# A layer kernel's paired FFN products: a weight split ahead of the last product, another order at the last job's end, sums on GpSimd, and two small products from parts

## The chip, the cores and the metric

The kernel runs on one core of one Trainium2 chip. The metric is the device time in microseconds (us) of one execution. The engines of a core are called PE (TensorE, matrix products), DVE (VectorE), ACT (ScalarE), POOL (GpSimd) and SP (SyncE, which here only issues loads and stores). Each engine works through its own list of instructions in order, and waits where an instruction needs another engine's result. SBUF is the memory of 128 partitions that the engines work on; PSUM has eight banks, in which products add up.

## The reference

One layer of a streaming encoder, on x of 512 rows by 1024 columns in float32:

```python
def swiglu(x, w1, w3, w2):
    return (jax.nn.silu(x @ w1) * (x @ w3)) @ w2

f = swiglu(rms_norm(h, ffn1_pre_g), ffn1_w1, ffn1_w3, ffn1_w2)       # FFN 1
h = h + 0.5 * rms_norm(f, ffn1_post_g)
u = rms_norm(h, mix_pre_g)
...                                   # the mixer: recurrent branch, attention with a
bias = table[t5_bucket(j - 128 - i)]  # relative bias from a table of 32 x 16, gates, w_o
...
f = swiglu(rms_norm(h, ffn2_pre_g), ffn2_w1, ffn2_w3, ffn2_w2)       # FFN 2
h = h + 0.5 * rms_norm(f, ffn2_post_g)
```

w1 and w3 are 1024 x 2816, w2 is 2816 x 1024. 2816 columns are 22 blocks of 128.

## The kernel before, in words

**Products from parts.** Float32 products are made from two parts. `split2` (L191) writes a high part by an ACT copy to the type float32r (L193, "whi" or "hT" in the profile), and the low part as the difference on DVE (L194, "wlo"). A product then is three float32r matmuls: high by high, low by high, high by low. Weights that need no more than that are split by `split_to` (L151), whose lines are L158 (ACT) and L159 (DVE). Loads go by SP, in the order of one long list of weights (`dma_one`, L139). There are 42 buffers of 4 KB a partition, "slots"; a slot is taken again when its last reader is done.

**Pairs of blocks.** The first blocks of w1 and w3 (4 of each in FFN 1, 2 of each in FFN 2) are plain products with 512 columns, L203 to L205. All others go through the class `Pairs` (L476 to L606). One job takes two blocks of w1 (name w1a in FFN 1, w1b in FFN 2) or of w3 (w3a, w3b), as a 2 x 2 matrix of halves, and makes it with 7 products where plainly there are 8. FFN 1 has 18 such jobs, FFN 2 has 20; jobs of w1 and w3 take turns, w1 first. One of the 7 products, `mm_s` (L464), is 12 matmuls with 256 columns (L471 to L473). The 7 need sums of the weights' quarters a11, a12, a21, a22 (and sums of x, made once, t1 to t4):

- S12: two sums (L517, L518), made by POOL, from a21, a22, a11
- S34: two sums (L522, L523), made by DVE, from a12 and S12, and from a11 and a21

The method `prep(m, i)` issues the preparation of job m in five steps: 0 the two sums of S12; 1 the split of the first block, which has a11 and a12; 2 the sums of S34 and the split of S12, which gives s1 and s2; 3 the split of S34, which gives s3 and s4; 4 the split of a22. A step that was already issued is left out when it is called again.

**The order inside a job.** `run` (L534) writes the order by hand. In job n, PE makes a11, s1, then a22 of the job before (function `last`, L591), s2, a12 (c11, L565), s4, s3. Between them stand the copies out of PSUM on ACT (L550, L553, L559, L579, into the tile "ct") and adds on DVE (L568, L573, L580, L585, L586), and the next job's preparation: prep(n+1, 1) right behind `last`, prep(n+1, 2) behind s2, prep(n+1, 3) behind s4, prep(n+1, 4) and prep(n+2, 0) at the job's end. `last` of a w1 job in FFN 1 also copies out of PSUM on ACT (L594) and multiplies the whole job by the norm's factor Rb on DVE (L595); the silu (L596) follows behind s4's add. Rb is handed to `Pairs` in FFN 1 alone (`self.R`); in FFN 2 the norm's factor is in x already. `last` of a w3 job ends with one product on DVE (L603).

In the last job, c11 is made behind s3, and ahead of it `tail()` is called, behind s2: it splits the first two tiles of the hidden layer (`hid.to`, "hT") and the first two blocks of w2, in turn, ACT before DVE in each. In FFN 1 `silu()` of that job comes behind s4, as in the others.

**Two small products.** `root` and `factor` (L708, L714) make Rb: the rows' 512 factors are put on four diagonals (DVE, L712, "dgs") and spread over all partitions by products of float32 ones with them (L717). It stands between plain products of FFN 1. `bias_in` and `bias_rows` (L725, L730) make the bias rows from the table: POOL loads a one-hot matrix 32 x 384 and the table 32 x 16 in job 1, and in job 3 one float32 product (L733) gives 16 x 384, which ACT copies out (L735, "erow"). Such additions to the jobs are handed in as `hooks`, by job and place. Two tiles named gap and gap2 hold memory and are not used.

Of the kernel before, what the change touches and what calls it, by code (L numbers as in the profile page):

```python
# [15 lines left out]
P = 128  # L16
# [6 lines left out]
N_HEADS = 16  # L23
# [28 lines left out]
def hybrid_layer(ctx: ExitStack, tc: tile.TileContext, a: dict, out: bass.AP):  # L52
# [32 lines left out]

    veps = cp.tile([P, NT], F32, name="veps")

    cp.tile([P, 172], F32, name="gap")
    sm.tile([P, 256], F32, name="gap2", bufs=1)
    uT = cp.tile([P, 2, KT, SEQ], F32R, name="uT")  # L90


# [383 lines left out]
    class Pairs:  # L476
# [14 lines left out]
        def prep(self, m, i, eng=None):  # L491
            if m >= len(self.jobs) or (m, i) in self.ready:
                return
            self.ready.add((m, i))
            k = self.k0 + 2 * m
            if i == 0:
                if k not in loaded or k + 1 not in loaded:
                    self.raws(m)
                s12, s34 = slot([P, 2 * QH], name="S12"), slot([P, 2 * QH], name="S34")
                self.w[m] = {"r": (raws.pop(k), raws.pop(k + 1)), "s": (s12, s34)}  # L500
            W = self.w[m]
            (ra, rb), (s12, s34) = W["r"], W["s"]
            a11, a12, a21, a22 = ra[:, :QH], ra[:, QH:], rb[:, :QH], rb[:, QH:]

            def both(src, w=2 * QH):
                hi = slot([P, w], F32R, name="whi")
                lo = slot([P, w], F32R, name="wlo")
                split2(hi, lo, src)
                return hi, lo

            def halves(p, a, b):
                W[a] = p[0][:, :QH], p[1][:, :QH]
                W[b] = p[0][:, QH:], p[1][:, QH:]

            if i == 0:
                e = eng or pool
                e.tensor_tensor(out=s12[:, :QH], in0=a21, in1=a22, op=ALU.add)  # L517
                e.tensor_tensor(out=s12[:, QH:], in0=s12[:, :QH], in1=a11, op=ALU.subtract)  # L518
            elif i == 1:
                halves(both(ra), "a11", "a12")  # L520
            elif i == 2:
                dve.tensor_tensor(out=s34[:, QH:], in0=a12, in1=s12[:, QH:], op=ALU.subtract)  # L522
                dve.tensor_tensor(out=s34[:, :QH], in0=a11, in1=a21, op=ALU.subtract)  # L523
                halves(both(s12), "s1", "s2")
            elif i == 3:
                halves(both(s34), "s3", "s4")
            elif i == 4:
                t = slot([P, 2, QH], F32R, name="w22")
                split2(t[:, 0, :], t[:, 1, :], a22)
                W["a22"] = t[:, 0, :], t[:, 1, :]  # L530
            if all((m, x) in self.ready for x in range(5)):
                del W["r"], W["s"]

        def run(self, tail, hooks={}):  # L534
            X = self.X
            assert st["get"] == st["split"] == self.k0, (st, self.k0)
            st["get"] = st["split"] = self.k0 + 2 * len(self.jobs)
            last = silu = lambda: None
            for n, (nm, f) in enumerate(self.jobs):
                W = self.w.pop(n)  # L540
                first = nm == self.na
                tmp = slot([P, 4, 256], name="ct")
                q1, q5, u, v = (tmp[:, i, :] for i in range(4))
                c = slot([P, 2, SEQ], name="cc")
                if first:
                    self.c1[f] = c
                bu, bx, bc = (bank("c")[:, :256] for _ in range(3))
                at = lambda i: [f() for f in hooks.get((n, i), ())]
                mm_s(W["a11"], X["b11"], bu)
                act.activation(q1, bu, AF.Copy)  # L550
                at(1)
                mm_s(W["s1"], X["t1"], bx)
                act.activation(q5, bx, AF.Copy)  # L553
                at(2)
                silu = last() or silu
                self.prep(n + 1, 1)
                mm_s(W["s2"], X["t2"], bu, True)
                del W["s1"], W["s2"]
                act.activation(u, bu, AF.Copy)  # L559
                at(3)  # L560
                if n == len(self.jobs) - 1:
                    tail()
                self.prep(n + 1, 2)

                def c11():  # L565
                    mm_s(W["a12"], X["b21"], bc)
                    del W["a11"], W["a12"]
                    dve.tensor_tensor(out=c[:, 0, :256], in0=bc, in1=q1, op=ALU.add)  # L568

                if n < len(self.jobs) - 1:  # L570
                    c11()
                mm_s(W["s4"], X["b22"], bx, True)
                dve.tensor_tensor(out=c[:, 0, 256:], in0=bx, in1=u, op=ALU.add)  # L573
                self.prep(n + 1, 3)
                silu()
                silu = lambda: None
                mm_s(W["s3"], X["t3"], bu, True)
                del W["s3"], W["s4"]
                act.activation(v, bu, AF.Copy)  # L579
                dve.tensor_tensor(out=c[:, 1, 256:], in0=v, in1=q5, op=ALU.add)  # L580
                if n == len(self.jobs) - 1:
                    c11()
                if not first:
                    c1 = self.c1[f]
                    dve.tensor_tensor(out=c1[:, 0, :], in0=c1[:, 0, :], in1=c[:, 0, :], op=ALU.mult)  # L585
                    dve.tensor_tensor(out=c1[:, 1, 256:], in0=c1[:, 1, 256:], in1=c[:, 1, 256:], op=ALU.mult)  # L586
                self.prep(n + 1, 4)
                self.prep(n + 2, 0)
                self.raws(n + 3)

                def last(W=W, bu=bu, c=c, f=f, first=first):  # L591
                    mm_s(W.pop("a22"), X["t4"], bu, True)
                    if first and self.R is not None:
                        act.activation(c[:, 1, :256], bu, AF.Copy)  # L594
                        dve.tensor_tensor(out=c, in0=c, in1=self.R, op=ALU.mult)  # L595
                        return lambda: act.activation(c, c, AF.Silu)  # L596
                    if first:
                        act.activation(c[:, 1, :256], bu, AF.Silu)
                        act.activation(c[:, 0, :], c[:, 0, :], AF.Silu)
                        act.activation(c[:, 1, 256:], c[:, 1, 256:], AF.Silu)  # L600
                    else:
                        c1 = self.c1.pop(f)
                        dve.tensor_tensor(out=c1[:, 1, :256], in0=bu, in1=c1[:, 1, :256], op=ALU.mult)  # L603
                        self.hid.f += [c1[:, 0, :], c1[:, 1, :]]

            last()  # L606
# [47 lines left out]
    dma_one(pairs_a.k0)  # L654
    dma_one(pairs_a.k0 + 1)
    make_identity(nc, ident)
    ones = slot([P, P], name="ones")
    pool.memset(ones, 1.0)
    ps = [bank("f") for _ in range(NS)]

    def split_first(u, kp):
# [34 lines left out]
    def t_split(n):  # L696
        X1[f"t{n + 1}"] = to_slots(tg[n])

    dgs = slot([P, NT, P], name="dgs")

    s4 = small(NT, "s4")

    def squares():
        for t in range(NT):
# [3 lines left out]
    def root():  # L708
        r = rstd4(s4)
        act.activation(tiny, tiny, AF.Silu)  # L710
        for t in range(NT):
            dve.tensor_scalar(out=dgs[:, t, :], in0=ident, scalar1=r[:, t : t + 1], scalar2=NEWT, op0=ALU.mult, op1=ALU.mult)  # L712

    def factor():  # L714
        psr = bank("r")
        for t in range(NT):
            pe.matmul(psr[:, t * P : (t + 1) * P], ones, dgs[:, t, :], start=True, stop=True)  # L717
        for i in range(2):
            act.activation(Rb[:, i, :], psr, AF.Copy)

# [2 lines left out]
    oh, erow = [], []  # L723

    def bias_in():  # L725
        oh.append(slot([N_BUCKETS, NREL + 1 + N_HEADS], name="oh"))
        pool.dma_start(out=oh[0][:, : NREL + 1], in_=a["onehot"])
        pool.dma_start(out=oh[0][:, NREL + 1 :], in_=a["rel_bias"])

    def bias_rows():  # L730
        pse = bank("e")
        t = oh.pop()
        pe.matmul(pse[:N_HEADS, : NREL + 1], t[:, NREL + 1 :], t[:, : NREL + 1], start=True, stop=True)  # L733
        erow.append(slot([N_HEADS, NREL + 1], name="erow"))
        act.activation(erow[0], pse[:N_HEADS, : NREL + 1], AF.Copy)  # L735

# [60 lines left out]
    def swiglu(f):  # L797
        t = gates.pop(f)
        hid.f.append(silu_mul(t[:, 0, :], ps[2 * f + 1], t))
# [20 lines left out]
    point(True)  # L820
    xg.clear()
    tg.clear()
    late = {(0, 1): [lambda: swiglu(2)], (0, 3): [lambda: gate(3)], (1, 1): [bias_in, lambda: swiglu(3)], (3, 1): [bias_rows]}
    for i in range(P // 16):
        late[4 + i, 1] = [lambda i=i: bias_spread(i)]

    def w2_ahead():
        hid.to(1)
        split_to(st["split"] + 1)
        hid.to(2)  # L830
        split_to(st["split"] + 1)

    pairs_a.run(w2_ahead, late)
# [460 lines left out]
```

## Time and profile before

| | us |
|---|---|
| median of 3 runs | 1136.61 (1136.0 to 1136.88) |
| profiled execution | 1137.54 |
| its span on the core | 1135.5 |
| PE busy | 1125.4 (99%) |
| DVE busy | 790.0 (70%) |
| ACT busy | 597.8 (53%) |
| POOL busy | 241.1 (21%) |

The page gives the busy time of each engine; PE's clock was granted at nine tenths or more in all of its 40 slices. All times of instructions in this document are counted in us from the span's start. The pairs of FFN 1 stand at about 50 to 237, those of FFN 2 at about 800 to 1005.

A line of the instructions in order of time has the start, the duration, the engine, the line of the program, the operation, what it writes and reads, the shape, and in brackets how long the engine stood idle before it and what ended that. A matmul's record is longer than the step to the next one, because products overlap: a product of 256 columns follows another 0.12 us after it, one of 512 columns 0.227 us. On the other engines the records overlap a little too: an ACT copy of 128 x 1024 lasts 1.06 us as a record and gives way to the next after 0.95; for DVE's subtraction of that size the two are 1.21 and 1.14, for a DVE sum of 128 x 512 they are 0.68 and 0.6.

### The profile page before, as it was taken

To read this page: it belongs to the slowest core of one execution; us is meant where nothing else is said; L and a number is where in the kernel's file an instruction comes from. 1 tells how busy PE (TensorE), PEld (TensorE's weight loads), DVE (VectorE), ACT (ScalarE), POOL (GpSimd) and SP (SyncE) were. 2 spreads that over 40 slices of the span, in tenths; PEclk is the share of its full clock that TensorE was granted. 3 is DMA by queue.
4 is the path that set the end of the run, shared out by engine and by line. 5 is a ranking of instruction groups with operands and counts; after the bars stand their busy time and mean duration, and the time that the engine had idled before them with its cause. 6 is when DMAs were issued, how large, how long until landed. Compare 5 with 4: busy or idle time off the path is not lost.

```text
span 1135.5 us, 17456 instructions
## 1 busy us (share of the span) xinstructions
PE 1125.4 (99%) x6835; PEld 1006.0 (89%) x6835; DVE 790.0 (70%) x1252; ACT 597.8 (53%) x1060; POOL 241.1 (21%) x203
## 2 busy tenths in 40 slices
PE   9999999999999999999999999999999999999997
PEld 7899999988888987888888888889999999998886
DVE  5898989885336747695678865767787777885313
ACT  7755655574324349944656653356555555573211
POOL 0035444200000000001555641000533233300000
PEclk9999999999999999999999999999999999999999
DMA  9235563264313411234122333531333332265101
GB/s 324 96 103 137 122 150 113 75 222 151 110 56 130 149 57 56 75 94 148 56 80 89 93 102 103 187 109 39 111 101 99 100 112 94 74 195 176 38 19 56
DMA packets 37139, 124.95 MB, mean 110 GB/s; under 512 B 4529, under 2 KB 6449, under 8 KB 37057
## 3 DMA queue, kind: packets, MB, share of 16 engines
q1 hardware_dynamic: 34272, 115.15, 30.8%
q0 software_dynamic: 2640, 8.43, 3.8%
q8 instruction: 53, 0.87, 0.3%
q10 hardware_dynamic: 144, 0.26, 0.1%
q14 instruction: 30, 0.24, 0.1%
HBM read 116.50 MB, written 7.33 MB: 109 GB/s over the span
## 4 chain that ended last, share of the span: by engine, by line
PE 91%; DVE 5%; ACT 3%; issue 1%; DMA 0%; SPq 0%; DVEq 0%; ACTq 0%
PE c L472 10%; PE f L203 10%; PE f L204 10%; PE f L205 10%; PE c L473 10%; PE c L471 10%; PE acc L222 8%; PE acc L223 8%; PE acc L221 8%; DVE wlo L194 2%; PE pt L1097 1%; PE s L1061 1%; PE s L1060 1%; DVE S L523 1%; PE tr L313 1%
## 5 line engine op out<-in xcount | busy, mean ns | idle before, releaser
L203 PE MATMUL f<-uT,whi 128*128 128x512 f32 (+1 forms) x472 | 171.7, 364 | 0.0
L204 PE MATMUL f<-uT,wlo 128*128 128x512 f32 (+1 forms) x472 | 170.4, 361 | 0.1
L205 PE MATMUL f<-uT,whi 128*128 128x512 f32 (+1 forms) x472 | 170.1, 360 | 0.0
L221 PE MATMUL acc<-whi,hT 128*128 128x512 f32 x352 | 137.1, 390 | 0.0
L222 PE MATMUL acc<-wlo,hT 128*128 128x512 f32 x352 | 137.0, 389 | 0.0
L223 PE MATMUL acc<-whi,hT 128*128 128x512 f32 x352 | 136.9, 389 | 0.0
L472 PE MATMUL c<-Xh,wlo 128*128 128x256 f32 x456 | 129.8, 285 | 1.1 <-DVE wlo L194 0.6
L471 PE MATMUL c<-Xh,whi 128*128 128x256 f32 x456 | 129.1, 283 | 0.0
L472 PE MATMUL c<-uT,wlo 128*128 128x256 f32 x456 | 129.0, 283 | 0.0
L471 PE MATMUL c<-uT,whi 128*128 128x256 f32 x456 | 129.0, 283 | 0.0
L473 PE MATMUL c<-uT,whi 128*128 128x256 f32 x456 | 129.0, 283 | 0.0
L473 PE MATMUL c<-Xl,whi 128*128 128x256 f32 x456 | 129.0, 283 | 0.0
L193 ACT ACTIVATE whi<-S 128x1024 fp32r<-128x1024 f32 x76 | 80.2, 1057 | 53.0 <-DVE S L523 53.0
L194 DVE TENSOR_TENSOR wlo<-S,whi 128x1024 fp32r<-128x1024 f32 x76 | 101.9, 1341 | 0.3 <-ACT whi L193 0.3
L203 PEld LDWEIGHTS f<-uT,whi 128*128 128x128 f32 x472 | 89.1, 189 | 14.5 <-issue 1.4
L204 PEld LDWEIGHTS f<-uT,wlo 128*128 128x128 f32 x472 | 89.2, 189 | 13.8 <-DVE wlo L159 0.9
L205 PEld LDWEIGHTS f<-uT,whi 128*128 128x128 f32 x472 | 89.1, 189 | 13.5
L472 PEld LDWEIGHTS c<-Xh,wlo 128*128 128x128 f32 x456 | 87.5, 192 | 2.4 <-DVE wlo L194 2.4
L471 PEld LDWEIGHTS c<-Xh,whi 128*128 128x128 f32 x456 | 87.5, 192 | 0.6 <-ACT ct L550 0.6
L471 PEld LDWEIGHTS c<-uT,whi 128*128 128x128 f32 x456 | 87.5, 192 | 0.0
L472 PEld LDWEIGHTS c<-uT,wlo 128*128 128x128 f32 x456 | 87.5, 192 | 0.0
L473 PEld LDWEIGHTS c<-uT,whi 128*128 128x128 f32 x456 | 87.5, 192 | 0.0
(312 smaller groups left out, 2646.8 us busy)
## 6 DMA issues: line engine op xcount, KB each, us to landing
raw_w2a<-in_w2a_dram SPq DMA_DIRECT2D x22, 512.0 KB, 4.4
raw_w1b<-in_w1b_dram SPq DMA_DIRECT2D x22, 512.0 KB, 3.9
raw_w3b<-in_w3b_dram SPq DMA_DIRECT2D x22, 512.0 KB, 4.0
raw_w2b<-in_w2b_dram SPq DMA_DIRECT2D x22, 512.0 KB, 4.4
raw_w3a<-in_w3a_dram SPq DMA_DIRECT2D x21, 512.0 KB, 4.5
raw_w1a<-in_w1a_dram SPq DMA_DIRECT2D x20, 512.0 KB, 4.3
raw_wg<-in_wg_dram SPq DMA_DIRECT2D x16, 512.0 KB, 4.0
raw_xr<-in_xr_dram SPq DMA_DIRECT2D x8, 512.0 KB, 4.0
```

The lines of the kernel that those rows point to most:

```text
L193: act.activation(hi, src, AF.Copy)
L194: dve.tensor_tensor(out=lo, in0=src, in1=f32(hi), op=ALU.subtract)
L203: pe.matmul(ps[:, c0:c1], wh[:, s], h_, start=k == 0, stop=False)
L204: pe.matmul(ps[:, c0:c1], wl[:, s], h_, start=False, stop=False)
L205: pe.matmul(ps[:, c0:c1], wh[:, s], l_, start=False, stop=k == KT - 1)
L221: pe.matmul(acc[n], x[:, 0, c], wh[:, s], start=first, stop=False)
L222: pe.matmul(acc[n], x[:, 0, c], wl[:, s], start=False, stop=False)
L223: pe.matmul(acc[n], x[:, 1, c], wh[:, s], start=False, stop=last)
L313: pe.transpose(ps[:, k * P : (k + 1) * P], hg[:, kk * P : (kk + 1) * P], ident)
L471: pe.matmul(ps, wh[:, s], xh, start=first, stop=False, skip_group_check=True)
L472: pe.matmul(ps, wl[:, s], xh, start=False, stop=False, skip_group_check=True)
L473: pe.matmul(ps, wh[:, s], xl, start=False, stop=k == 3, skip_group_check=True)
```

## The change

1. In FFN 1, prep(n+1, 1), the split of the next job's first block, is issued behind L553, ahead of `last`, and no longer behind it.
2. In the last job, `silu()` is called ahead of `tail()`, and `tail()` is called twice, each time for one tile of the hidden layer and one block of w2: once at the old place, once behind v's add (L580) ahead of c11. The silu is FFN 1's alone, the second call is in both FFNs.
3. In FFN 2, the sums of S34 are issued on POOL, in step 0 of the preparation, behind S12's; in FFN 1 they stay on DVE in step 2. 40 instructions change engine.
4. The factor's product is made in float32r from a high and a low part of the row factors, with 8 diagonals for 4, as two products with 512 columns. The bias product is made likewise, from parts of the table that are split at a new place, behind s2 of job 2 (`bias_parts`).

```diff
-    cp.tile([P, 172], F32, name="gap")
-    sm.tile([P, 256], F32, name="gap2", bufs=1)
+    cp.tile([P, 168], F32, name="gap")
+    sm.tile([P, 240], F32, name="gap2", bufs=1)
...
+            def sums34(e):
+                e.tensor_tensor(out=s34[:, QH:], in0=a12, in1=s12[:, QH:], op=ALU.subtract)
+                e.tensor_tensor(out=s34[:, :QH], in0=a11, in1=a21, op=ALU.subtract)
+
             if i == 0:
                 e = eng or pool
                 e.tensor_tensor(out=s12[:, :QH], in0=a21, in1=a22, op=ALU.add)
                 e.tensor_tensor(out=s12[:, QH:], in0=s12[:, :QH], in1=a11, op=ALU.subtract)
+                if self.R is None:
+                    sums34(e)
             elif i == 1:
                 halves(both(ra), "a11", "a12")
             elif i == 2:
-                dve.tensor_tensor(out=s34[:, QH:], in0=a12, in1=s12[:, QH:], op=ALU.subtract)
-                dve.tensor_tensor(out=s34[:, :QH], in0=a11, in1=a21, op=ALU.subtract)
+                if self.R is not None:
+                    sums34(dve)
                 halves(both(s12), "s1", "s2")
...
                 at(2)
+                if self.R is not None:
+                    self.prep(n + 1, 1)
                 silu = last() or silu
                 self.prep(n + 1, 1)
...
                 if n == len(self.jobs) - 1:
+                    silu()
+                    silu = lambda: None
                     tail()
...
                 if n == len(self.jobs) - 1:
+                    tail()
                     c11()
...
-    ones = slot([P, P], name="ones")
-    pool.memset(ones, 1.0)
+    ones = slot([P, P], F32R, name="ones")
+    pool.memset(f32(ones), 1.0)
...
-    dgs = slot([P, NT, P], name="dgs")
+    dgs = [slot([P, NT, P], F32R, name="dgs") for _ in range(2)]
...
+    tiny_r = [sm.tile([P, NT], F32R, tag="smr", name=f"rn{n}", bufs=2) for n in range(2)]
...
-        for t in range(NT):
-            dve.tensor_scalar(out=dgs[:, t, :], in0=ident, scalar1=r[:, t : t + 1], scalar2=NEWT, op0=ALU.mult, op1=ALU.mult)
+        rh, rl = tiny_r
+        dve.tensor_scalar(out=rh, in0=r, scalar1=NEWT, scalar2=None, op0=ALU.mult)
+        dve.scalar_tensor_tensor(out=rl, in0=r, scalar=NEWT, in1=f32(rh), op0=ALU.mult, op1=ALU.subtract)
+        for x, d_ in zip(tiny_r, dgs):
+            for t in range(NT):
+                dve.tensor_scalar(out=d_[:, t, :], in0=ident, scalar1=f32(x)[:, t : t + 1], scalar2=None, op0=ALU.mult)
...
-        for t in range(NT):
-            pe.matmul(psr[:, t * P : (t + 1) * P], ones, dgs[:, t, :], start=True, stop=True)
+        for n, d_ in enumerate(dgs):
+            pe.matmul(psr, ones, d_.rearrange("p t q -> p (t q)"), start=n == 0, stop=n == 1)
...
-        oh.append(slot([N_BUCKETS, NREL + 1 + N_HEADS], name="oh"))
+        oh.extend((slot([N_BUCKETS, NREL + 1 + N_HEADS], name="oh"), slot([N_BUCKETS, NREL + 1 + 2 * N_HEADS], F32R, name="ohr")))
...
+    def bias_parts():
+        t, u = oh
+        n = NREL + 1
+        hi, lo = u[:, n : n + N_HEADS], u[:, n + N_HEADS :]
+        act.activation(u[:, : n + N_HEADS], t, AF.Copy)
+        dve.tensor_tensor(out=lo, in0=t[:, n:], in1=f32(hi), op=ALU.subtract)
+        oh[:] = [hi, lo, u[:, :n]]
...
-        pe.matmul(pse[:N_HEADS, : NREL + 1], t[:, NREL + 1 :], t[:, : NREL + 1], start=True, stop=True)
+        pe.matmul(pse[:N_HEADS, :n], hi, u, start=True, stop=False)
+        pe.matmul(pse[:N_HEADS, :n], lo, u, start=False, stop=True)
...
-    late = {(0, 1): [lambda: swiglu(2)], (0, 3): [lambda: gate(3)], (1, 1): [bias_in, lambda: swiglu(3)], (3, 1): [bias_rows]}
+    late = {(0, 1): [lambda: swiglu(2)], (0, 3): [lambda: gate(3)], (1, 1): [bias_in, lambda: swiglu(3)], (2, 3): [bias_parts], (3, 1): [bias_rows]}
...
     def w2_ahead():
-        hid.to(1)
-        split_to(st["split"] + 1)
-        hid.to(2)
+        hid.to(hid.done + 1)
         split_to(st["split"] + 1)
```

More of the change, by code (lines that the diff above doesn't have):

```diff
@@ L725, in bias_in @@
     def bias_in():
-        oh.append(slot([N_BUCKETS, NREL + 1 + N_HEADS], name="oh"))
+        oh.extend((slot([N_BUCKETS, NREL + 1 + N_HEADS], name="oh"), slot([N_BUCKETS, NREL + 1 + 2 * N_HEADS], F32R, name="ohr")))
         pool.dma_start(out=oh[0][:, : NREL + 1], in_=a["onehot"])
         pool.dma_start(out=oh[0][:, NREL + 1 :], in_=a["rel_bias"])
+    def bias_parts():
[5 more added lines that the diff above has]
+        oh[:] = [hi, lo, u[:, :n]]
     def bias_rows():
         pse = bank("e")
-        t = oh.pop()
-        pe.matmul(pse[:N_HEADS, : NREL + 1], t[:, NREL + 1 :], t[:, : NREL + 1], start=True, stop=True)
+        hi, lo, u = oh
+        oh.clear()
+        n = NREL + 1
+        pe.matmul(pse[:N_HEADS, :n], hi, u, start=True, stop=False)
+        pe.matmul(pse[:N_HEADS, :n], lo, u, start=False, stop=True)
         erow.append(slot([N_HEADS, NREL + 1], name="erow"))
```

## The prediction

> **What bounds the kernel now.** I read four views in this order: the page (busy times, chain), the waits of the two FFN 1 and FFN 2 stretches, the instructions in order of time around TensorE's pauses, and the stretches by engine.
>
> One line of the page, then waits of two windows, 60 to 240 and 800 to 1005 (waiter, what it waited for, total us, times, longest):
>
> ```profile
> PE 1125.4 (99%) x6835; PEld 1006.0 (89%) x6835; DVE 790.0 (70%) x1252; ACT 597.8 (53%) x1060; POOL 241.1 (21%) x203
> DVE cc L595 <- ACT cc L594: 17.5, 9, 3.1
> PE c L472 <- DVE wlo L194: 0.6, 1, 0.6
> PE c L471 <- ACT ct L579: 0.3, 1, 0.3
> DVE wlo L194 <- ACT whi L193: 38.0, 10, 4.7
> ```
>
> TensorE (PE) is the bound, and only what shortens its stream counts. The second to fourth of the five lines are FFN 1's, the last is FFN 2's. Busy time hides short pauses, because a product's record overlaps the next one. So I take the steps between starts: a 256-column product follows the last by 0.12 us, a 512-column one by 0.227. Wherever a step is longer, time is lost:
>
> ```profile
> 93.12 0.28 PE L471 MATMUL c<-Xh,whi 128*128 128x256 f32 x1
> 93.49 0.39 PE L472 MATMUL c<-Xh,wlo 128*128 128x256 f32 x1
> 93.72 0.28 PE L473 MATMUL c<-Xl,whi 128*128 128x256 f32 x1
> ...
> 234.07 0.28 PE L473 MATMUL c<-uT,whi 128*128 128x256 f32 x1
> 234.66 0.39 PE L471 MATMUL c<-Xh,w 128*128 128x256 f32 x1 [0.31 <-ACT ct L579]
> 234.88 0.28 PE L472 MATMUL c<-Xh,w 128*128 128x256 f32 x1
> ```
>
> At 93.12 two steps take 0.60 instead of 0.24: 0.36 lost, waiting for the low half of the next job's s1. The same stands at 113.62, 134.14 and 154.65: together 1.43. At 234.07, 0.57 is lost. At 61.06 (job 1's s1) 0.85, at 967.71 and 988.09 (FFN 2) 0.22 and 0.34. These are all the pauses over 0.05 in the pair stretches beside the two small products:
>
> ```profile
> 38.98 0.39 PE L205 MATMUL f<-uT,whi 128*128 128x512 f32 x1
> 39.20 1.05 PE L717 MATMUL r<-dgs,ones 128*128 128x128 f32 x8
> 40.01 0.48 PE L203 MATMUL f<-uT,whi 128*128 128x512 f32 x1
> 40.33 0.40 PE L204 MATMUL f<-uT,wlo 128*128 128x512 f32 x1
> 40.56 0.39 PE L205 MATMUL f<-uT,whi 128*128 128x512 f32 x1
> ```
>
> From 38.98 to 40.56 three ordinary steps should take 0.68; they take 1.58, so the factor costs 0.90. The bias product's two L733 records stand between 256-column products that start at 81.98 and 83.28: 1.30 where three ordinary steps would take 0.36, so it costs 0.94.
>
> **Next job's split ahead of the last product (FFN 1).** The chain to the pause at 93.12, on VectorE (DVE):
>
> ```profile
> 86.53 1.23 DVE L595 TENSOR_TENSOR cc<-cc,Rb 128x1024 f32<-128x1024 f32 x1 [2.46 <-ACT cc L594]
> 87.67 2.33 DVE L194 TENSOR_TENSOR wlo<-raw_w1a,whi 128x1024 fp32r<-128x1024 f32 x1
> 89.92 1.78 DVE L522 TENSOR_TENSOR S<-raw_w1a,S 128x512 f32<-128x512 f32 x1
> 91.63 0.68 DVE L523 TENSOR_TENSOR S<-raw_w1a,raw_w1a 128x512 f32<-128x512 f32 x1
> 92.23 1.21 DVE L194 TENSOR_TENSOR wlo<-S,whi 128x1024 fp32r<-128x1024 f32 x1
> ...
> 972.37 4.16 POOL L517 TENSOR_TENSOR S<-raw_w1b 128x512 f32<-128x512 f32 x1 [6.76 <-PE c L472]
> ```
>
> DVE stands idle 2.46 before L595, since L595 needs ScalarE's (ACT's) L594, which needs the last product a22. Then it has no gap to the end. The change puts the split whi (0.95 per step on ACT) behind L553, which starts at 84.68, so at 85.06. That ends at 86.1, and DVE can begin wlo at 86.1 instead of L595 at 86.53. The work behind is the same: wlo 1.14, L595 1.14, two sums 0.6 each, wlo 1.14, and 2.2 of blocking by GpSimd (POOL), 6.85 in all, so it ends at 92.95 instead of 93.4. The pause needs it by 93.24, which leaves 0.3. At 113.62 the gain is 106.5 against 107.04, likewise enough. What is late behind it: L595, L594's bank and the silu L596 move back by up to 0.7; L596 began only at 93.36, five us after L595, and no bank waits. Value -1.43; ends 0 (GpSimd's blocks fall worse and take the 0.45) and -1.43. In the other jobs L603 and the split only change places, and DVE's wait of 17.5 in all is their cover.
> The moved split issues no DMA, and it passes no POOL instruction; SP's order of loads is the same.
>
> The pause at 61.06 stays: its split belongs to job 0, which has no last product ahead of it. DVE has no gap from 42.42 to it but 0.1. Value 0; ends +0.3 and -0.85.
>
> **The last job.** At 234.07 the last product waits for v (L579), which stands on ACT behind hT, whi, hT, whi and the silu, 230.35 to 234.24. Now silu (0.95), hT (0.52) and whi (0.95) stand ahead: 232.77. s3 ends at 232.75, so v is done at 233.2, before c11's end at 234.19. The second hT and whi follow, on ACT until 234.7, on DVE until 236.4; TensorE wants them after c11, a22 and the first 12 products of FFN 1's w2, at 232.75 + 1.44 + 1.44 + 2.72 = 238.4. That is the cover, two us. Value -0.57; ends -0.57 and 0. FFN 2's tail has no pause before, and the same two us of cover: 0.
>
> **Small products.** The factor becomes two 512-column steps, 0.45 instead of 0.90. But DVE builds eight diagonals (0.20 a step) for four, and two 128x4 operations (0.20 each by the neighbouring L251 to L253): 1.2 more from 36.02. It stood idle 0.92 before 37.82, so it falls 0.28 behind, and the split at 42.42, bound by ACT before, by DVE now, gains only 0.30. As DVE has no gap from there to 61.06, that counts: -0.30; ends -0.45 and 0. The bias product becomes two of 384 columns, between 0.12 and 0.227: 0.17 each, 0.35 for 0.94. Value -0.55, for what changing shapes costs; ends -0.59 and 0. Its parts take ACT about 0.5 (erow took 0.48) and DVE 0.16 in job 2, whose table landed at 63.3, thirteen us ahead; DVE then waits for ACT until 77.3, behind it the two sums and s1's split, due at 82.2 and done at 81.3 at the latest.
>
> **FFN 2's sums by GpSimd.** DVE loses 40 instructions of 0.60 a step, 24 us; POOL gains 40 of 1.29 (alone) to 4.16. DVE's operation blocked by a POOL sum takes 1.1 longer (L522 1.78 for 0.68); in 820 to 978 I count 15.3 us of such lengthening for 32 sums, 0.48 each. So DVE gets 24 back and loses 19 to 44, and had 38 us of idle in this stretch (140.2 busy of 178): it does not become the bound. At the pauses its chain shortens: at 962.9 the split of a1, then L522 1.78, L523 0.68 and s1's split, until 967.8. Without the sums, and with POOL's L518 and one added sum blocking 1.1 each, s1's split ends at 966.65. Value -0.56, both pauses; ends -0.56, and the cost in the fourth rival.
> By the Trainium skill, "SBUF — State Buffer", section "Who interferes with whom", a VectorE operation with two SBUF inputs and a GpSimd one that reads SBUF lock each other out for a whole instruction. The rows of 1.1 agree, but only in about every second case; with the rule in every case DVE loses the 44, still less than its idle time, and the sum stays.
> S34 must be there when ACT splits it, at 987.35 for job 18. POOL began that job's sums at 972.37; with two more at the mean of the four rows, 1.84, it ends at 982.5. New waits for S34 on load slots lie over eight us ahead. Two queues are passed. POOL's later sums start later; the only POOL load behind them is FFN 2's gain (L260), issued at 1064.64 and until then 78.5 behind DVE, so it has cover. SP's loads get their slots up to 3 us later (867.83 is one issue) and take 4 to land: about 875, where POOL reads from 877.28. These 2 us are the cover; behind them stands POOL's lead of 4.8 over ACT's split (982.5 to 987.35).
>
> **Sum.** -1.43 - 0.57 - 0.30 - 0.55 - 0.56 = -3.41. The profiled execution took 1137.54 (span 1135.5 and 2.04 around it), so 1134.1; it lies 0.93 above the median of 1136.61, and against that median the forecast is 1133.2.
>
> **Rivals.**
> 1. As summed: 1133.2, from 1132.4 to 1134.2 by factor and bias at either end. For it: every pause has a named last waiter that the edit moves. Chance 0.58.
> 2. Job 1's 0.85 goes too: 1132.3. POOL's L517 at 57.79 slips in just before DVE's L523 at 57.84 and blocks it 1.1; a shift of 0.1 changes who goes first. Against it: both follow TensorE. Chance 0.12.
> 3. The early split gains nothing: DVE was already gapless behind L595, and 0.3 of margin is less than one block of 1.1. The four pauses stay: 1134.6, the same by the bound below. Chance 0.17.
> 4. POOL becomes late, slower. A job gives it 10.08. If its four sums go at 4.16 and three times 2.16, 10.64, it falls back 0.56 a job; the 4.8 of lead is gone after 8.6 jobs, and the other 11.4 lose 6.4: 1136.6 - 2.9 + 6.4 = 1140.1. It decides from 2.5 us a sum; the rows' mean is 1.84. Chance 0.08.
> The Trainium skill's "GPSIMD Engine Reference", "Performance versus the Vector engine", speaks against this move: elementwise work there takes about twice as long. Here 1.30 against 0.68 agrees.
> The rest, 0.05, are mixtures near no change.
>
> **Numbers.** A measurement of this kernel tells 0.2% (2.3 us) from no change: faster is below 1134.3. From 1 nearly all and 2: 0.69 faster; 3, the rest and 1's edge: 0.23 same; 4: 0.08 slower. The range leaves out rival 4 and the outermost edges: 1131.6 (rival 2 with both small products at their best) to 1136.0 (rival 3 with the small products at nothing and part of FFN 2's gain lost).
>
> **What would show it.** DVE's wait before L595 shrinks from 17.5 to under 9, and steps at job 4, 6, 8 and 10's s1 are 0.12. v in the last job starts within 0.2 of s3's end. The factor's record shows two products in 0.45, the bias two in 0.35. POOL's busy time rises by 40 times 1.3 to 2.2, and ACT's split of S34 never waits for POOL. Wrong it would be if pauses over 0.1 stand in FFN 2's jobs with a POOL sum behind them, or new ones in FFN 1's even jobs.

## The result, and the profile after

The changed kernel takes 1132.7 us, median of 7 runs (1132.33 to 1133.73), against 1136.53 of the kernel before in the same series (1135.89 to 1136.88). The ratio is 0.9968, with a 95% interval of 0.9957 to 0.998: faster by 0.32%. The forecast was 1133.2, the range 1131.6 to 1136.0. The profiled execution of the changed kernel, with a span of 1132.0, was the slowest of the seven, 1133.73; why is told below.

The busy times on the page of the changed kernel (us, share of the span, instructions):

```profile
PE 1122.5 (99%) x6829; PEld 1005.0 (89%) x6829; DVE 798.0 (70%) x1219; ACT 597.4 (53%) x1061; POOL 302.9 (27%) x243
```

Its waits in the FFN 1 stretch, 60 to 240 (waiter, what it waited for, total us, times, longest):

```profile
DVE wlo L194 <- ACT whi L193: 12.0, 11, 2.2
...
DVE cc L606 <- ACT cc L605: 3.1, 1, 3.1
...
PE c L472 <- DVE wlo L194: 0.8, 1, 0.8
```

L606 is the multiplication by Rb (L595 before). DVE waited 17.5 us for its input in 9 jobs; now it waits there once, in the last job, where there is no next split. The waiting itself is mostly still there: 12.0 us of it now stand ahead of splits, for ACT's half, a wait that the list of the kernel before does not have. What counts is that the chain behind it starts earlier. Of TensorE's waits in that stretch one is left, job 1's. DVE has 33 instructions fewer and is busy 8 us longer.

The chain on DVE that leads to the place of the first of the four pauses, in the changed kernel, and then TensorE at that place, each in order of time:

```profile
85.27 1.23 DVE L194 TENSOR_TENSOR wlo<-raw_w1a,whi 128x1024 fp32r<-128x1024 f32 x1 [2.23 <-ACT whi L193]
86.42 1.22 DVE L606 TENSOR_TENSOR cc<-cc,Rb 128x1024 f32<-128x1024 f32 x1
87.55 1.78 DVE L516 TENSOR_TENSOR S<-raw_w1a,S 128x512 f32<-128x512 f32 x1
89.26 1.77 DVE L517 TENSOR_TENSOR S<-raw_w1a,raw_w1a 128x512 f32<-128x512 f32 x1
90.96 1.21 DVE L194 TENSOR_TENSOR wlo<-S,whi 128x1024 fp32r<-128x1024 f32 x1
```

```profile
92.35 0.28 PE L471 MATMUL c<-Xh,whi 128*128 128x256 f32 x1
92.47 0.28 PE L472 MATMUL c<-Xh,wlo 128*128 128x256 f32 x1
92.59 0.28 PE L473 MATMUL c<-Xl,whi 128*128 128x256 f32 x1
```

The split now stands ahead of the multiplication. The chain starts at 85.27, where it started at 86.53; TensorE is 0.77 ahead at this place, so DVE is 0.49 earlier against it. GpSimd's sums blocked other DVE operations than before (both sums, not the split of the first block and the first sum), but the total is the same, 2.2 us. The low half of s1 is done at 92.17 and is wanted at 92.47: the margin is 0.3. The steps are 0.12, with nothing lost.

The last job: the ACT instructions in order of time, then TensorE where it lost 0.57 before:

```profile
228.19 1.05 ACT L607 ACTIVATE cc<-cc 128x1024 f32<-128x1024 f32 x1
229.14 0.62 ACT L193 ACTIVATE hT<-sw 128x512 fp32r<-128x512 f32 x1
229.66 1.05 ACT L158 ACTIVATE whi<-raw_w2a 128x1024 fp32r<-128x1024 f32 x1
230.79 0.39 ACT L589 ACTIVATE ct<-c 128x256 f32<-128x256 f32 x1
```

```profile
231.91 0.28 PE L473 MATMUL c<-uT,whi 128*128 128x256 f32 x1
232.03 0.28 PE L471 MATMUL c<-Xh,w 128*128 128x256 f32 x1
232.15 0.28 PE L472 MATMUL c<-Xh,w 128*128 128x256 f32 x1
```

v (L589) starts as s3's last product ends, and its 0.39 are over 0.85 before TensorE goes on behind c11, at 232.03. No step is longer than 0.12.

The small products of the changed kernel on TensorE, the factor and then the bias:

```profile
38.76 0.39 PE L205 MATMUL f<-uT,whi 128*128 128x512 f32 x1
38.98 0.61 PE L733 MATMUL r<-dgs,ones 128*128 128x512 f32 x2
39.44 0.39 PE L203 MATMUL f<-uT,whi 128*128 128x512 f32 x1
```

```profile
81.52 0.28 PE L473 MATMUL c<-uT,whi 128*128 128x256 f32 x1
81.72 0.34 PE L759 MATMUL e<-ohr 32*16 32x384 f32 x1
81.92 0.33 PE L760 MATMUL e<-ohr 32*16 32x384 f32 x1
82.17 0.39 PE L471 MATMUL c<-Xh,whi 128*128 128x256 f32 x1
82.39 0.28 PE L472 MATMUL c<-Xh,wlo 128*128 128x256 f32 x1
82.51 0.29 PE L473 MATMUL c<-Xl,whi 128*128 128x256 f32 x1
```

The factor's two products take their two steps, 0.46 in all. The bias product costs 0.99 from 81.52 to 82.51, less three ordinary steps: 0.63 where it cost 0.94. Each change of shape, into the small products and out of them, still takes about 0.1 to 0.2 more than a step.

### The profile page after: what moved, and what is told of

Its sections match the earlier page's. It is cut to its first block, busy times and chain, and to the rows that moved or that the text cites. A ratio compares the mean times of both kernels' runs of the same rounds, so it can differ in the third digit from the quotient of the medians.

```text
span 1132.0 us, 17496 instructions
## 1 busy us (share of the span) xinstructions
PE 1122.5 (99%) x6829; PEld 1005.0 (89%) x6829; DVE 798.0 (70%) x1219; ACT 597.4 (53%) x1061; POOL 302.9 (27%) x243
## 4 chain that ended last, share of the span: by engine, by line
PE 91%; DVE 3%; ACT 2%; DMA 2%; issue 1%; SPq 0%; DVEq 0%
PE c L472 11%; PE c L471 11%; PE c L473 11%; PE f L204 10%; PE f L203 10%; PE f L205 9%; PE acc L221 8%; PE acc L222 8%; PE acc L223 8%; PE pt L1122 1%; DMA h<-in_x_dram 1%; DMA xt<-in_xT_dram 1%; DMA raw_w3a<-in_w3a_dram 1%; PE s L1086 1%; PE s L1085 1%
## 5 line engine op out<-in xcount | busy, mean ns | idle before, releaser
L203 PE MATMUL f<-uT,whi 128*128 128x512 f32 (+1 forms) x472 | 171.6, 364 | 0.0
L194 DVE TENSOR_TENSOR wlo<-S,whi 128x1024 fp32r<-128x1024 f32 x76 | 113.4, 1492 | 2.0 <-ACT whi L193 1.1
L203 PEld LDWEIGHTS f<-uT,whi 128*128 128x128 f32 x472 | 89.1, 189 | 14.6 <-issue 1.4
L205 PEld LDWEIGHTS f<-uT,whi 128*128 128x128 f32 x472 | 89.1, 189 | 13.5
L193 ACT ACTIVATE whi<-S 128x1024 fp32r<-128x1024 f32 x76 | 77.9, 1055 | 22.2 <-DVE S L517 22.2
```

What stands on the lines that cost most here:

```text
L193: act.activation(hi, src, AF.Copy)
L194: dve.tensor_tensor(out=lo, in0=src, in1=f32(hi), op=ALU.subtract)
L203: pe.matmul(ps[:, c0:c1], wh[:, s], h_, start=k == 0, stop=False)
L205: pe.matmul(ps[:, c0:c1], wh[:, s], l_, start=False, stop=k == KT - 1)
```

## The experiments

For the four parts, and for one run further down, I also give how long TensorE takes from a product early in s1 of job 1, behind the pause there, to its last product. This leaves out the kernel's start, job 1's pause and the end behind the last product, which differ from one execution to the next. It is 1065.43 in the kernel before and 1062.67 in the changed one.

**Each part alone.** The kernel before, with one part of the change at a time. The early split:

```diff
                 at(2)
+                if self.R is not None:
+                    self.prep(n + 1, 1)
                 silu = last() or silu
```

> Of the four parts only the early split in FFN 1 is made. My theory: the four pauses at the first products of s1 (93, 114, 134, 155) go by themselves, since what made s1's low half late was DVE's wait for the last product's copy: 4 x 0.35 = 1.4 us less, so 1135.1 against 1136.5, and DVE's wait before the multiplication by Rb falls from 17.5 to about 3 us. Rival: the pauses go only together with another part (the shift of 0.4 us that the small products give to all that follows moves GpSimd's blocks out of the way): then two or more of the four stay at about 0.3 each, and the time is 1136.0 to 1136.5. The pause at 61 stays at 0.85, and those at 234, 968 and 988 stay, by both.

FFN 2's sums on GpSimd (`sums34(e)` in step 0 where R is None, as in the change):

> Only FFN 2's sums of S34 go to GpSimd. My theory: the pauses at 968 and 988 (0.22 and 0.34 by the steps between starts) go, the rest stays, so 0.5 us less: 1136.0. DVE's busy time between 800 and 978 does not fall, although 36 operations leave it; it rises from 140 to about 149 us, since GpSimd's 72 sums block it instead of 36, and this costs nothing because DVE had idle time. Rival: the pauses went by the earlier parts' shift of 2.7 us and GpSimd's sums only cost: then the pauses stay or new ones come in FFN 2's jobs, 1136.5 to 1138.

The last job's order (`silu()` ahead of `tail()`, `tail()` in two parts):

> Only the last job's order is changed (the silu first, the tail in two parts). My theory: the pause of 0.57 at 234 goes, nothing else changes: 1136.0. Rival: the second part of the tail, now behind v, comes late for the w2 products: a pause of 0.3 to 0.6 at about 238 takes its place, 1136.5.

The small products from parts:

> Only the two small products are made from parts. My theory, from the trace of the changed kernel: the factor's place costs 0.43 instead of 0.90 and the bias product's 0.63 instead of 0.94, and job 1's pause at 61 takes back 0.2, so 0.6 us less: 1135.9. If the 0.2 at 61 is not due to them (PE comes 0.66 earlier there, DVE only 0.45), the pause stays at 0.85 and the time is 1135.7. Rival: the bias parts delay DVE in job 2 enough to widen the pause at 93 by 0.2 or more: 1136.1 or above.

The four shared one series, with the kernel before at 1136.37, median of 33 runs:

| part alone | median | against before | between s1 of job 1 and the last product |
|---|---|---|---|
| early split | 1134.82 | -1.55 | 1064.03 (-1.40) |
| FFN 2's sums | 1136.05 | -0.32 | 1064.87 (-0.56) |
| last job | 1135.83 | -0.54 | 1065.39 (-0.04) |
| small products | 1135.80 | -0.57 | 1065.23 (-0.20: the bias product -0.31, the pause at 91 +0.06, the rest in steps of 0.02 and less); the factor, ahead of this stretch, -0.46 |

The early split's ratio is 0.9987 (0.9978 to 0.9996), clear of 1; the other three have 1 inside their intervals, so each of them is read from the trace. The four pauses go by the early split alone, and L595's wait falls to 3.1. Both FFN 2 pauses go by the sums alone. The last job's pause goes too; that profile gained only 0.04 because another pause, 0.48 at 761, ahead of the first transpose in front of FFN 2, stood in that execution and in none of the others. The bias parts widened no pause by more than 0.06. The rivals of all four fall. What two of the expectations say of job 1's pause fell too: it did not stay at 0.85 with the early split (0.42), and with the small products alone it was neither 0.85 nor 0.2 longer than in the kernel before, but 0.21. The four medians together give -2.98, less than the whole change; with an interval of about 1 us to either side of each, that difference tells nothing.

**Job 1's pause.** In the profiled runs so far it was anything from 0.2 to 1.07, in kernels that do the same there (counted by the steps; those that an expectation below calls 0 have 0.21 to 0.24). So two runs of the changed kernel took away what was suspected, beside the changed kernel itself once more:

> The changed kernel once more, as the one to compare with on this chip. 1132.7; the single runs lie in two groups, some at 1132.3 to 1132.9 and some about a microsecond higher, as job 1's pause is there or not.

One multiplication on DVE is moved behind s1's split:

```diff
-    late = {(0, 1): [lambda: swiglu(2)], (0, 3): [lambda: gate(3)], (1, 1): [bias_in, lambda: swiglu(3)], (2, 3): [bias_parts], (3, 1): [bias_rows]}
+    late = {(0, 1): [lambda: swiglu(2)], (1, 1): [bias_in, lambda: gate(3), lambda: swiglu(3)], (2, 3): [bias_parts], (3, 1): [bias_rows]}
```

> The changed kernel, and gate(3), a 0.6 us multiplication on DVE, moves from job 0 to job 1, behind s1's split. My theory of job 1's pause (0 in four profiled runs, 0.3 in one, 0.85 and 1.07 in two): DVE has no gap ahead of s1's split, and two of its operations are blocked 1.1 each if job 2's first weight lands after about 56, because GpSimd's two sums then fall on DVE's second sum and on s1's split. With 0.6 less ahead, DVE is through with s1's split by 60.3 at the worst, so the pause is at most 0.3 in the profile, and the highest single runs fall from 1133.7 to 1133.0 or less; median 1132.4 to 1132.7. Rival: the pause is due to the late landing alone, DVE's work does not matter: the pause and the spread stay, and 0.6 of DVE work in job 1 costs 0 to 0.3 at the next s1.

Job 2's sums of S12 are made by DVE, behind job 1's splits, in place of GpSimd:

```diff
-                self.prep(n + 2, 0)
+                self.prep(n + 2, 0, dve if self.R is not None and n == 0 else None)
```

> The changed kernel, and job 2's two S12 sums are made by DVE, behind job 1's splits, and not by GpSimd. My theory: without GpSimd's two sums nothing blocks DVE ahead of job 1's s1, whose split is done at about 59.2, over 1 us ahead of need: the pause is 0 in every run, whenever the weight lands; single runs lie within 0.6 of each other, median 1132.3 to 1132.6. Rival (the load itself is late for something PE needs): the pause stays in some runs. Price: 1.2 us more on DVE in job 1, whose wait of 3.1 before the multiplication by Rb covers it; if not, a pause of up to 0.5 at the next s1 (71).

Medians 1132.51, 1132.77 and 1132.52. The five runs of the changed kernel lie between 1132.35 and 1132.89: the second group that was expected a microsecond higher did not come here. With the sums on DVE the chain to s1 of job 1 has no blocked operation:

```profile
56.64 0.68 DVE L516 TENSOR_TENSOR S<-raw_w3a,S 128x512 f32<-128x512 f32 x1
57.24 0.68 DVE L517 TENSOR_TENSOR S<-raw_w3a,raw_w3a 128x512 f32<-128x512 f32 x1
57.84 1.22 DVE L194 TENSOR_TENSOR wlo<-S,whi 128x1024 fp32r<-128x1024 f32 x1
```

Its pause is 0.00, and at the next s1 a step is 0.05 too long, no more (0.04 in the kernel before). Its single runs lie 0.67 apart, against the 0.6 expected. The profiled execution of the changed kernel, which has 1.06, shows the other end; these are DVE's and then GpSimd's instructions of it:

```profile
56.80 0.68 DVE L516 TENSOR_TENSOR S<-raw_w3a,S 128x512 f32<-128x512 f32 x1
57.40 1.78 DVE L517 TENSOR_TENSOR S<-raw_w3a,raw_w3a 128x512 f32<-128x512 f32 x1
59.10 2.31 DVE L194 TENSOR_TENSOR wlo<-S,whi 128x1024 fp32r<-128x1024 f32 x1
```

```profile
56.94 1.69 POOL L521 TENSOR_TENSOR S<-raw_w1a 128x512 f32<-128x512 f32 x1 [55.49 <-DMA raw_w1a<-in_w1a_dram]
58.71 1.63 POOL L522 TENSOR_TENSOR S<-S,raw_w1a 128x512 f32<-128x512 f32 x1
```

GpSimd starts when job 2's weight has landed, 0.14 to 0.26 later in all 11 profiles in which it makes these sums; that load took 4.4 to 6.3 us from issue to landing. Each of the two sums here holds up the DVE operation that comes behind it by 1.1. What counts is when that is, against DVE's first sum. In these 11 executions:

| GpSimd's first sum against DVE's first | executions | job 1's pause |
|---|---|---|
| 0.47 to 1.26 earlier | 8 | 0.21 to 0.42 |
| 0.26 earlier | 1 | 0.63 |
| 0.14 and 0.55 later | 2 | 1.06 and 0.85 |

So this pause is neither the edit's nor fixed; in these runs it hangs on the landing of one load in the execution. Moving the multiplication by itself gave nothing here: in that execution the load was early, and the pause 0.21, as in the changed kernel beside it, while the multiplication came to stand in the way of job 2's s1, a new pause of 0.31 at 70. The rival's price was about right, and my median missed by 0.07. What it would do with a late landing, no run shows.

**FFN 2's sums, or the early split there.** The changed kernel, with `self.prep(n + 1, 1)` ahead of `last` in both FFNs, and S34's sums on DVE in both:

> The changed kernel, but in FFN 2 the sums of S34 stay on DVE and instead the early split is made there too. My theory: the two pauses at 965 and 985 are of the same kind as FFN 1's, a chain on DVE that starts too late; the early split starts it at least 0.95 earlier, so they go as well: 1132.7, the same as the changed kernel, while DVE's busy time between 800 and 975 goes back from 149 to about 140 and GpSimd's from 120 to 64. Rival: in FFN 2 the chain is limited by GpSimd's blocks (the sum of 1.78), and by ACT's three silu pieces behind the last product: the pauses stay at 0.2 and 0.3, 1133.2.

1132.8, and both pauses are gone (their stretch is 1062.65, as the changed kernel's 1062.67). So either edit removes them. The forecast of the busy times fell: between 800 and 978 DVE has 152.8 rather than 140, and GpSimd 50.9 rather than 64.

**How much more GpSimd bears.** The changed kernel with one, and with two of S34's sums made twice in FFN 2:

```diff
                 if self.R is None:
                     sums34(e)
+                    e.tensor_tensor(out=s34[:, :QH], in0=a11, in1=a21, op=ALU.subtract)
```

> The changed kernel with one sum more per job on GpSimd in FFN 2: the second sum of S34 is made twice, with the same result. It measures how far GpSimd is from becoming late. My theory: a sum takes 1.71 on average there (119.9 us for 70 sums in the stretch 800 to 978); five take 8.6 of a job's 10.08, so GpSimd still has time left, and the time is that of the changed kernel, 1132.5 to 1132.9. Rival: what counts is not the mean but the sums' order against DVE's work; the delayed S34 makes ACT's split late, and pauses of 0.2 to 1 come in many of the 20 jobs: 1135 to 1145.

```diff
                 if self.R is None:
                     sums34(e)
+                    sums34(e)
```

> The changed kernel with two sums more per job on GpSimd in FFN 2: both sums of S34 are made twice, with the same result. My theory: six sums at 1.71 take 10.3 of 10.08, so GpSimd falls behind by 0.2 to 0.5 a job after its lead of some 8 us is used up; with 20 jobs that stays near the edge: 1132.5 to 1137, with GpSimd busy over 95% of the stretch and ACT's splits of S34 waiting for it. Rival (GpSimd has half of its time free, since its durations shrink when DVE is less busy): 1132.5, no waits. Rival of the other sign: each sum blocks DVE by 1.1, DVE becomes the bound: 1140 or more.

1140.68 and 1154.93: the ratios to the kernel before are 1.0037 (1.0024 to 1.005) and 1.0161 (1.0148 to 1.0175). My times fell in both. With two sums more, the rival that makes DVE the bound stands. With one, the rival's time holds and so does its word on the order against DVE's work, but not its path, a late S34 that ACT waits for: GpSimd is busy 154.9 of the 178 us, and no ACT split waits for it. But DVE, in order of time ahead of the first pause:

```profile
824.30 1.52 DVE L591 TENSOR_TENSOR cc<-ct 128x256 f32<-128x256 f32 x1
825.74 1.78 DVE L597 TENSOR_TENSOR cc<-cc,cc 128x512 f32<-128x512 f32 x1
827.44 1.52 DVE L598 TENSOR_TENSOR cc<-cc,cc 128x256 f32<-128x256 f32 x1
828.88 1.78 DVE L194 TENSOR_TENSOR w<-raw_w1b,w 128x512 fp32r<-128x512 f32 x1
```

```profile
831.41 0.28 PE L471 MATMUL c<-uT,whi 128*128 128x256 f32 x1
832.94 0.39 PE L472 MATMUL c<-uT,wlo 128*128 128x256 f32 x1 [1.25 <-DVE wlo L194]
```

Each of DVE's operations there, 0.41 or 0.68 by itself, is 1.1 longer, the small ones of 256 columns as well as the large. DVE becomes the bound before GpSimd is late. With two sums more GpSimd is busy 175.0 of 178, and ACT waits for S34 too, 13.5 us in 8 places.

The number of GpSimd's sums, and of DVE operations that are over 0.4 longer than the shortest of their kind in any of these kernels, between 800 and 978:

| kernel | GpSimd's sums, mean us | DVE operations blocked | DVE busy |
|---|---|---|---|
| before | 35, 1.84 | 19 | 140.2 |
| sums on DVE, early split | 34, 1.50 | 29 | 152.8 |
| changed | 69, 1.72 | 52 | 149.4 |
| one sum more | 84, 1.85 | 78 | 168.7 |
| two more | 93, 1.91 | 91 | 175.2 |

This table shows one half of the matter; the other half is GpSimd's own waiting. These are DVE's instructions in the kernel before beside GpSimd's sum of 4.16 that the prediction shows (972.37 to 976.53):

```profile
972.96 0.68 DVE L522 TENSOR_TENSOR S<-raw_w3b,S 128x512 f32<-128x512 f32 x1
973.56 0.68 DVE L523 TENSOR_TENSOR S<-raw_w3b,raw_w3b 128x512 f32<-128x512 f32 x1
974.16 1.21 DVE L194 TENSOR_TENSOR wlo<-S,whi 128x1024 fp32r<-128x1024 f32 x1
975.30 0.41 DVE L568 TENSOR_TENSOR cc<-c,ct 128x256 f32<-128x256 f32 x1
975.63 0.41 DVE L573 TENSOR_TENSOR cc<-c,ct 128x256 f32<-128x256 f32 x1
975.96 1.65 DVE L194 TENSOR_TENSOR wlo<-S,whi 128x1024 fp32r<-128x1024 f32 x1
```

Three operations with two inputs in SBUF run at their own length, and the sum, 1.29 by itself, ends 1.16 after the third (975.37): here GpSimd waits. Two adds with one input in PSUM (L568, L573) run inside the sum and are no longer for it; the next split, with two inputs in SBUF, waits for the sum's end (1.65 for 1.21). I take the last part of each record, as long as that operation is by itself, as the time in which it works. Then in none of the 13 profiles does a DVE operation with two SBUF inputs work beside a sum of GpSimd for more than 0.2 us (1170 sums in the pairs of both FFNs), while operations with a PSUM input do so 558 times. So one of the two always waits, and the table counts only the cases in which it is DVE.

That gives an estimate of the room there is: DVE's operations with two SBUF inputs, at their own steps (1.14, 0.6 and 0.33 us by size), and 1.11 for each sum of GpSimd (1.52 for 0.41 above) add up to 145 of the 178 us before, 161 in the changed kernel, 174 with one sum more and 178 with two. The last is the whole stretch. No run tests this sum by itself.

**All in one.** Job 2's sums on DVE, and the early split in FFN 2 in place of the sums on GpSimd:

> What the runs point to, in one kernel: the changed kernel with job 2's S12 sums on DVE (job 1's pause gone whenever the load lands), and with the early split in FFN 2 too in place of its sums of S34 on GpSimd. My theory: no pause over 0.05 in any job of both FFNs; 1132.3 to 1132.7, the same as the changed kernel's fast executions, without the executions a microsecond above. Rival: the two interact at the entry of FFN 2 or in job 2, and a pause of 0.2 to 0.3 stays: 1132.8.

1132.77 (1132.3 to 1133.05), 0.07 above what was expected, with no pause in any job. That is the changed kernel's time, within what the runs can tell; nothing is left to gain in the pairs from these two.

## Why the prediction was right, point by point

| term | forecast | traces |
|---|---|---|
| early split | -1.43 | -1.40 |
| last job | -0.57 | -0.57 |
| factor | -0.30 | -0.46 |
| bias | -0.55 | -0.31 |
| FFN 2's sums | -0.56 | -0.56 |
| sum | -3.41 | -3.30 |

The traces' column is put together from the runs of each part and the pauses; in the changed kernel's own profile the stretch and the factor give 3.22.

- **Early split.** Forecast: DVE begins 0.45 earlier and has 0.3 left at the pause. It began 0.49 earlier and had 0.3. The price of the blocks, 2.2 a job, was taken over from the rows before without a reason why it should stay; it did, though other operations paid it. The rival that it gains nothing is out, by the run of this part alone.
- **Last job.** As forecast; what came behind, the second half of the tail, was not late.
- **Factor, too small.** The step that failed is that DVE falls 0.28 behind by the added diagonals and gives up a part of the gain. The diagonals cost it nothing: the two small operations and the eight diagonals filled DVE's idle 0.92 and ended as ACT's copy did, at 38.0. How much earlier DVE's split at 42.42 came is another matter. Counted from the first product of L203, it stood at 19.54 before, at 19.33 in the profiled execution of the changed kernel, where DVE's row factors already came 0.37 late, and at 19.04 in the run of the small products alone, where it waits for ACT as before. So the gain there is 0.21 in one and 0.50 in the other. The -0.46 is what TensorE saves at the factor itself; how much of it job 1's pause takes back cannot be read, since that pause differs from one execution to the next.
- **Bias, too large.** Sized 0.35 for two steps between those of 256 and 512 columns; it measured 0.63, within the ends that were given. What was left out is the change of shape, which a step between equal products does not show.
- **FFN 2's sums.** Both pauses went, at the time foreseen: ahead of 965, s1's split ended at 964.02 (961.70 and 2.32); the forecast of 966.65 less the 2.68 gained by then is 963.97. In the stretch 800 to 978, 34 of the 40 operations moved. DVE got back some 20 and lost 28.5 by longer operations (47.5 of lengthening against 19.0); for all 40 that would be 24 and 34, inside the 19 to 44. The low end was a little off: between 820 and 978 the trace has 16.0 us of lengthening for 30 sums, 0.53 each and not 0.48. And 44 is less than DVE's idle time only if the 24 that it gets back are added to the 38.
- **Every second case.** The prediction read the lock between the two engines as met in about every second case. That reading is wrong: between 800 and 978 in the kernel before, 21 of the 35 sums hold up a DVE operation, 7 others only wait themselves, and 7 meet no operation with two SBUF inputs and take no more than 1.3 us. Adds that read one input from PSUM (L578, L583) stayed at their 0.41 after the change, while L590, with both inputs in SBUF, rose from 0.67 to 0.93 on average. By the Trainium skill, "SBUF — State Buffer", section "Who interferes with whom", a VectorE operation with two SBUF inputs contends with a GpSimd one that reads SBUF, by an exclusive lock, and one with at most one SBUF input does not. The trace agrees in every sum.
- **GpSimd late, the rival.** It did not come: in the changed kernel no ACT split waits for GpSimd. Its mechanism was wrong too. It was put at 2.5 us a sum, with GpSimd as the one that is late. The runs show the edge at less than one sum more per job, at a mean of 1.85, and DVE as the engine that is late. The chance of 0.08 was given to something much nearer than it looked.
- **Job 1's 0.85, the other rival.** Told as a matter of 0.1 in who goes first. The order is what counts, but over a span of about one microsecond, and in these runs the load decides it, not the edit.
- **The range.** Its low end does not follow from the terms. Rival 2 with both small products at their best is 1133.2 - 0.85 - 0.15 - 0.04, about 1132.2 and not 1131.6; rival 1 by itself runs from 1133.0, not from 1132.4. The 1132.7 lies in the wider range all the same, but 0.3 below what rival 1's terms allow.
- **Against the median.** The medians moved by 3.83, and by 3.95 in the later series, 0.5 to 0.65 more than the traces' sum. The two profiled executions can be taken apart. They differ by 3.81: 3.22 are the parts; the start (the first product of L203 at 22.88 and 22.66) and job 1's pause (0.85 and 1.06) cancel; 0.33 stand behind TensorE's last product, where the span's end comes 7.45 and 7.12 after that product's start, though every instruction up to the issue of the last store takes the same time; and 0.25 stand outside the span (2.03 and 1.78 around it). In the kernel before and the four parts that end took 7.2 to 7.5, in the changed kernel, its second run and the six kernels made from it 7.0 to 7.1; the chips differ too, and no run separates the two. For the medians the start (22.1 to 22.9 in the 13 profiles) and the pause count as well, since the profiled execution of the kernel before was a late one in both. How much of the 0.5 each of these makes up is argued, not shown.

## What to carry to other kernels

Where the bounding engine is 99% busy, list the steps between its starts, not its busy time: the few that are too long name the chains that are worth an edit, and what each is worth, to a tenth or two of a microsecond. Work that is given to GpSimd beside DVE is paid twice where DVE's operations read both inputs from SBUF: DVE's operations grew by 0.8 us for each sum that the change moved, and by 1.7 for each that one sum more per job added. So add up what of both engines cannot overlap, and ask how much more would tip it: this kernel was one sum per job away from a loss of 8 us against itself. And before explaining a difference of a microsecond between two profiles, look for a place that differs between executions of the same kernel.

## What the runs showed that I had not expected

- By the count above, DVE's operations with two SBUF inputs and GpSimd's sums never worked side by side, in 1170 sums. Where DVE was not held up, GpSimd waited or nothing stood beside it.
- One half-width sum more per job on GpSimd costs 8.2 us in 20 jobs (1140.68 against 1132.51), though GpSimd stays at 87% and TensorE at 97% of that stretch.
- Moving 34 operations off DVE in that stretch made it busier: 149.4 for 140.2 us between 800 and 978. And DVE's work paid more for the same sums when only its order changed: 152.8 with 34 sums on GpSimd and DVE's operations all kept, blocked 29 times instead of 19.
- Eight float32r diagonals and two small operations on DVE, 1.9 us where four diagonals took 0.9, cost nothing, while two products of 16 rows by 384 columns on TensorE cost 0.63.
